# Inverse norms of the MLA latents: diagonal tiles made one or two products ahead of the matmuls that spread them

## The chip, the core and the metric

The kernel runs on one core of one Trainium2 chip. The metric is the device time of one launch in microseconds (us). The engines named here are PE (matrix multiply), DVE (vector), ACT (scalar), POOL (GpSimd) and SP, whose queue issues most of the DMAs. Each works through its own list of instructions in order and waits for the others by semaphores.

## The reference, cut to what matters

The program is one layer of a hybrid decoder over 1024 tokens of width 2048. An RMSNorm and one input projection feed three head groups: multi-head latent attention (MLA), native sparse attention (NSA) and cross-attention into 256 memory tokens. Their outputs go through SiLU gates, one output projection, the residual and a last RMSNorm.

What the change touches is a small piece of it. The projection yields two latents of 512 features per token, `c_q` and `c_kv`, and each is normalised before it is multiplied by its up-projection:

```python
def rmsnorm(x, g):
    xf = x.astype(jnp.float32)
    y = xf * lax.rsqrt(jnp.mean(xf * xf, axis=-1, keepdims=True) + EPS)
    return (y * g.astype(jnp.float32)).astype(x.dtype)

q = (rmsnorm(c_q, q_norm_g) @ w_uq).reshape(...)
kv = (rmsnorm(c_kv, kv_norm_g) @ w_ukv).reshape(...)
```

## The kernel before, in words

**The projection.** Activations lie transposed: 128 features on the partitions, 1024 tokens along the row. The projection is done in 20 units of two feature tiles each, twice (once for each half of the 2048 input rows, so 40 units `u`; the second half starts at `u0` = 20). A unit is a Strassen-like scheme of seven products `s` = 0..6. A product is 12 matmuls of 512 columns: four k-tiles, each three times, because every operand is split in a high and a low float32r part (`mm3`, L124 to L126). `wprep` makes the split weights of a product two products ahead in the units around the change: ACT writes the high part (L118), DVE the low one (L112), and POOL forms sums of weight blocks (L719 to L723). `evac` takes the product out of PSUM, by ACT (L756, L760) or DVE (L758 to L770). In the second half POOL then adds the first half's result by a DMA (`work<-part`).

**Work at the side.** Everything else is hung on the list of products with `at(u, s, ...)`: the functions given there are issued after product `s` of unit `u`. In this part the engines' lists keep the order in which the code issues instructions. Here that are a compression MLP for keys in 12 chunks (`kc_chunk`, matmuls into tile `J`, 66x384) and one for values in four (`vc_start`, `vc_prep`, `vc_chunk`, loads of `in_w1v`), and the norms of the latents.

**The norms.** `c_sum` adds up the squares of four feature tiles in `cacc[g]` (`g` = 0 for `c_q`, 1 for `c_kv`). `c_col` (`col_rsqrt`) lets PE sum them over the partitions by eight pairs of tiny matmuls with a matrix of ones (L202), and DVE and ACT turn the sums into 8 columns of inverse norms (L130 to L136): column `i` holds those of tokens 128i to 128i+127, one token on a partition. `c_spread` (`spread`) turns them back into a row that is the same on all partitions. For each column DVE multiplies the identity matrix by it, which gives a diagonal tile `dg` (L214), and PE multiplies ones by that tile (L215). A `dg` tile holds two diagonals, and there are two such tiles at a time. Four diagonals fill a PSUM tile `T` of 512 columns, ACT copies it (L216), and after both halves the row is stored (`rd[g]`), to be read again much later by `c_load`.

So `c_spread` of one latent is eight instructions on DVE and eight matmuls on PE in turn, all after one product: product 6 of unit `u0+4` for `c_q` and product 0 of unit `u0+7` for `c_kv`. The profile has two records for each of these matmuls. `spread` is used at two more places earlier in the program, for the input's and the memory's norms, which stay as they are.

Of the kernel before, what the change touches and what calls it, by code (L numbers as in the profile page):

```python
# [6 lines left out]
F32 = mybir.dt.float32  # L7
F32R = mybir.dt.float32r
AF = mybir.ActivationFunctionType
ALU = mybir.AluOpType  # L10
AX = mybir.AxisListType

P = 128
# [3 lines left out]
NQ = SEQ // P  # L17
# [35 lines left out]
def hybrid_block_kernel(ctx: ExitStack, tc, a, out):  # L53
    nc = tc.nc
    V, S, G, PE = nc.vector, nc.scalar, nc.gpsimd, nc.tensor

    cst = ctx.enter_context(tc.tile_pool(name="cst", bufs=1))
    sb = ctx.enter_context(tc.tile_pool(name="sb", bufs=1))
# [5 lines left out]
    def nm(s):  # L64
        uid[0] += 1
        return f"{s}_{uid[0]}"

    def big(dt=F32R):
        return sb.tile([P, 2048], dt, tag="big", bufs=16, name=nm("big"))
# [22 lines left out]
    def psT():  # L92
        return ps.tile([P, 512], F32, tag="T", bufs=2, name=nm("T"))
# [10 lines left out]
    def store(dst, src):  # L104
        nc.sync.dma_start(dst, src)
# [32 lines left out]
    def const(name, shape, dt=F32):  # L138
        t = cst.tile(shape, dt, tag=name, name=name)
        load(t, a[name])  # L140
        return t


    def dram(name, shape):
        return dr.tile(shape, F32, name=name)
# [5 lines left out]
    rd = [dram(f"r{j}", [P, SEQ]) for j in range(2)]  # L151
# [53 lines left out]
    def spread(dst, col, n, bank=None):  # L205

        for i0 in range(0, n, 4):
            t = (bank or psT)()
            m = min(4, n - i0)
            for j in range(i0, i0 + m, 2):  # L210
                dg = sb.tile([P, 256], F32, tag="og", bufs=2, name=nm("dg"))
                for i in (j, j + 1):
                    d = dg[:, (i - j) * P:(i - j) * P + P]
                    V.tensor_scalar(d, ident, col[:, i:i + 1], None, op0=ALU.mult)  # L214
                    PE.matmul(t[:, (i - i0) * P:(i - i0 + 1) * P], ones, d, start=True, stop=True)  # L215
            S.activation(dst[:, i0 * P:(i0 + m) * P], t[:, :m * P], AF.Copy)  # L216
# [114 lines left out]
    for c in range(8):  # L331
# [4 lines left out]
        for k in (2 * c, 2 * c + 1):  # L336
            g = ng[:, k:k + 1]
# [6 lines left out]
            else:  # L344
                xr = work()
                t = big()
                parts = [(t[:, :512], t[:, 1024:1536]), (t[:, 512:1024], t[:, 1536:])]
            if k == 0:
# [3 lines left out]
                ones = const("ones", [P, P])  # L352
                ident = const("ident", [P, P])
# [110 lines left out]
    def in_load(key):  # L464
        cmp_["in"] = slot(F32)[:, :1024]
        load(cmp_["in"], cmp_[key])
# [116 lines left out]
    cacc = {}  # L583
# [12 lines left out]
    ccol = {}  # L596

    def c_col(g):
        ccol[g] = small()
        col_rsqrt(ccol[g][:, :NQ], cacc[g], NQ, 512)  # L600

    def c_spread(g):
        spread(cacc[g], ccol[g], NQ)
        store(rd[g], cacc[g])

    def c_load(j):
        t = big(F32)
# [193 lines left out]
    def at(u, s, *fs):  # L801
        side.setdefault((u, s), []).extend(fs)
# [105 lines left out]
    for k in range(8):  # L908
        g = 28 + 13 * k
# [21 lines left out]
    u0 = NU  # L931
# [11 lines left out]
    for c in range(12):  # L943
# [7 lines left out]
        if c == 7:  # L951
            at(x // 7, x % 7, kc_rest)
    at(u0 + 4, 5, lambda: c_col(0))
    at(u0 + 4, 6, lambda: c_spread(0))
    at(u0 + 6, 4, w2_load)
    at(u0 + 6, 5, kc_mid)
    at(u0 + 6, 6, kc_mid2, lambda: in_load("vc"), lambda: c_col(1))
    at(u0 + 7, 0, lambda: c_spread(1))
    at(u0 + 7, 1, kc_end)
    at(u0 + 7, 0, lambda: vc_load(0))  # L960
    at(u0 + 7, 2, vc_start, lambda: vc_prep(0))
# [14 lines left out]
    for h in range(4):  # L976
        g = 64 + 18 * h
# [820 lines left out]
```

## Time and profile before

| | |
|---|---|
| median of 3 runs | 1905.29 us (1904.3 to 1909.41) |
| profiled execution, its own time | 1902.97 us |
| span of its trace, first to last instruction | 1901.2 us |
| PE busy | 1789.8 us, 94% of the span |
| DVE busy | 1319.8 us, 69% |
| ACT busy | 854.1 us, 45% |
| POOL busy | 320.3 us, 17% |
| mean clock granted to PE | 0.978 of full speed |

The trace is of one execution, and its own time is 2.3 us below the median of the runs. The share of busy time is an average over stages. PE counts as busy while a matmul is under way, whatever its clock. A granted clock of 1.00 is 2.4 GHz, and 0.50 is 1.2 GHz. In a row of the timeline the first two numbers are the start and the length in us. Matmuls overlap in the pipe, so that their pace is read from one start to the next, not from their length. What stands in brackets at a row's end is the time that the engine had idled before it and whose instruction ended that.

### The profile page before, as it was taken

The numbers are of one execution on the slowest core, as the hardware profiler recorded it, in microseconds if no ns is written. First come the engines' busy times: TensorE is split into PE (matmuls) and PEld (weight loads), VectorE is DVE, ScalarE is ACT, GpSimd is POOL, SyncE is SP. The second block draws the span as 40 slices with busy tenths as digits, with TensorE's granted clock in tenths as the row PEclk, the third lists the DMA queues.
The fourth block names the chain that finished last, engine by engine and source line by source line (L and its number), as shares of the span: only waits on it lengthen the run. The fifth ranks groups of instructions, "written<-read, shape, count | busy, mean of one in ns | idle before, by whom it ended". The sixth has DMA issues, their size and how long they took to land. (4 is left out here: it accounts for less than half of the span.)

```text
span 1901.2 us, 26461 instructions
## 1 busy us (share of the span) xinstructions
PE 1789.8 (94%) x9310; PEld 1525.8 (80%) x9310; DVE 1319.8 (69%) x2478; ACT 854.1 (45%) x1712; POOL 320.3 (17%) x433
## 2 busy tenths in 40 slices
PE   8899999999999889989897999999999999989996
PEld 7788878887777767778776898888999988877885
DVE  7976778877866545766664887868777783544777
ACT  8753222222434344534454666545455453222344
POOL 0002223223242213233231221200000000000020
PEclk9999999999999989999998999999999999999998
DMA  6564877786588558878988213442122144754564
GB/s 223 184 190 166 293 256 270 256 305 224 220 227 240 146 153 235 274 215 252 301 251 264 80 61 136 156 130 65 46 73 68 56 140 141 245 167 144 167 195 192
DMA packets 124930, 351.91 MB, mean 185 GB/s; under 512 B 15355, under 2 KB 39613, under 8 KB 121725
## 3 DMA queue, kind: packets, MB, share of 16 engines
q1 hardware_dynamic: 119037, 329.25, 51.4%
q0 software_dynamic: 5760, 20.97, 6.3%
q8 instruction: 73, 1.20, 0.3%
q14 instruction: 60, 0.49, 0.1%
HBM read 242.14 MB, written 108.02 MB: 184 GB/s over the span
## 5 line engine op out<-in xcount | busy, mean ns | idle before, releaser
L124 PE MATMUL S<-big,wh 128*128 128x512 f32 x1336 | 529.5, 396 | 23.1 <-DVE work L758 7.9
L125 PE MATMUL S<-big,wh 128*128 128x512 f32 x1336 | 526.6, 394 | 4.5 <-DVE big L112 4.5
L126 PE MATMUL S<-big,wh 128*128 128x512 f32 x1336 | 526.5, 394 | 1.4 <-DVE wh L112 1.2
L124 PEld LDWEIGHTS S<-big,wh 128*128 128x128 f32 x1336 | 254.7, 191 | 80.0 <-issue 12.1
L125 PEld LDWEIGHTS S<-big,wh 128*128 128x128 f32 x1336 | 254.8, 191 | 56.4 <-DVE big L112 6.0
L126 PEld LDWEIGHTS S<-big,wh 128*128 128x128 f32 x1336 | 253.9, 190 | 57.1 <-DVE wh L112 3.4
L112 DVE TENSOR_TENSOR wh<-wraw,wh 128x512 fp32r<-128x512 f32 (+2 forms) x226 | 201.2, 892 | 80.7 <-ACT wh L118 80.6
L118 ACT ACTIVATE wh<-wraw 128x512 fp32r<-128x512 f32 (+2 forms) x226 | 145.5, 659 | 92.7 <-PE S L126 44.8
L112 DVE TENSOR_TENSOR big<-wraw,big 128x1024 fp32r<-128x1024 f32 x56 | 73.9, 1320 | 104.6 <-ACT big L118 104.4
L719 POOL TENSOR_TENSOR wraw<-wraw 128x512 f32<-128x512 f32 x38 | 56.1, 1475 | 460.6 <-DMA wraw<-in_w_feat 415.8
L645 ACT ACTIVATE work<-S,st 128x512 f32<-128x512 f32 (+3 forms) x148 | 84.4, 572 | 86.4 <-DVE st L1096 35.2
L118 ACT ACTIVATE wh<-rs 128x512 fp32r<-128x512 f32 x80 | 50.2, 628 | 158.3 <-POOL rs L720 126.4
L112 DVE TENSOR_TENSOR wh<-rs,wh 128x512 fp32r<-128x512 f32 x80 | 62.7, 784 | 65.2 <-ACT wh L118 65.0
L118 ACT ACTIVATE big<-wraw 128x1024 fp32r<-128x1024 f32 x56 | 59.2, 1056 | 84.8 <-PE J L126 57.7
L124 PE MATMUL J<-big,wh 128*128 128x512 f32 x214 | 84.2, 393 | 0.7 <-ACT wh L118 0.7
L125 PE MATMUL J<-big,wh 128*128 128x512 f32 x214 | 84.1, 393 | 0.0
L126 PE MATMUL J<-big,wh 128*128 128x512 f32 x214 | 83.9, 392 | 0.0
L118 ACT ACTIVATE wh<-T 128x512 fp32r<-128x512 f32 (+2 forms) x112 | 53.0, 504 | 46.5 <-PE T L1161 29.5
L756 ACT ACTIVATE work<-S 128x512 f32<-128x512 f32 x40 | 23.8, 596 | 110.5 <-PE S L126 105.9
L112 DVE TENSOR_TENSOR wh<-T,wh 128x512 fp32r<-128x512 f32 (+2 forms) x112 | 61.5, 570 | 10.5 <-ACT wh L118 10.1
L1425 POOL MEMSET wh<- 128x128 f32 x64 | 13.8, 227 | 291.8 <-PE O L125 173.5
L1078 PE MATMUL S<-big,big 128*128 128x512 f32 (+2 forms) x144 | 52.9, 368 | 8.5 <-ACT wraw L645 8.5
(377 smaller groups left out, 4133.2 us busy)
## 6 DMA issues: line engine op xcount, KB each, us to landing
wraw<-in_w_feat SPq DMA_DIRECT2D x80, 512.0 KB, 5.3
part<-work SPq DMA_DIRECT2D x40, 512.0 KB, 3.9
work<-part POOLq DMA_DIRECT2D x40, 512.0 KB, 6.7
work<-og SPq DMA_DIRECT2D x72, 256.0 KB, 4.3
wh<-in_w_o SPq DMA_DIRECT2D x32, 512.0 KB, 7.2
t<-wh SPq DMA_DIRECT2D x32, 512.0 KB, 3.0
wraw<-t SPq DMA_DIRECT2D x32, 512.0 KB, 3.8
wraw<-in_w_o SPq DMA_DIRECT2D x24, 512.0 KB, 4.1
```

Of the source, the lines that this page charges most:

```text
L112: V.tensor_tensor(dst, src, f(hi), op=ALU.subtract)
L118: S.activation(hi, src, AF.Copy)
L124: PE.matmul(dst, sh, mh, start=start, stop=False, skip_group_check=shared)
L125: PE.matmul(dst, sh, ml, start=False, stop=False, skip_group_check=shared)
L126: PE.matmul(dst, sl, mh, start=False, stop=stop, skip_group_check=shared)
L645: S.activation(dst, src, AF.Exp, bias=m, scale=-1.0, accum_out=s)
L719: E.tensor_tensor(B12, B22, B12, op=ALU.subtract)
L756: S.activation(C21, B, AF.Copy)
L1078: PE.matmul(d, qm[0][:, c:c + P], km[0][:, k0:k0 + n], start=True, stop=False)
L1425: G.memset(f(t[:, o:o + P]), 0.0)
```

## The change

`c_spread` of the latents no longer calls `spread`. It is cut in two steps for each half of the row. `c_diag(g, half)` makes four diagonals in the two `dg` tiles. `c_spread(g, half)` multiplies ones by each `dg` tile as a whole (256 columns, one matmul in place of two of 128 columns) and copies the half row out. `c_spread(g, 0)` issues `c_diag(g, 1)` at its end, since the two `dg` tiles are free only then.

```diff
+    dgs = {}
+    def c_diag(g, half):
+        for j in (4 * half, 4 * half + 2):
+            dg = dgs[j] = sb.tile([P, 256], F32, tag="og", bufs=2, name=nm("dg"))
+            for i in (j, j + 1):
+                V.tensor_scalar(dg[:, (i - j) * P:(i - j) * P + P], ident, ccol[g][:, i:i + 1], None, op0=ALU.mult)
-    def c_spread(g):
-        spread(cacc[g], ccol[g], NQ)
-        store(rd[g], cacc[g])
+    def c_spread(g, half):
+        t = psT()
+        for j in (4 * half, 4 * half + 2):
+            PE.matmul(t[:, (j % 4) * P:(j % 4) * P + 256], ones, dgs.pop(j), start=True, stop=True)
+        S.activation(cacc[g][:, half * 512:half * 512 + 512], t, AF.Copy)
+        if half:
+            store(rd[g], cacc[g])
+        else:
+            c_diag(g, 1)
...
-    at(u0 + 4, 6, lambda: c_spread(0))
+    at(u0 + 4, 6, lambda: c_diag(0, 0))
+    at(u0 + 5, 0, lambda: c_spread(0, 0))
+    at(u0 + 5, 1, lambda: c_spread(0, 1))
...
-    at(u0 + 7, 0, lambda: c_spread(1))
+    at(u0 + 7, 0, lambda: c_diag(1, 0))
+    at(u0 + 7, 2, lambda: c_spread(1, 0))
+    at(u0 + 7, 4, lambda: c_spread(1, 1))
```

PE's list at the first place (`c_q`), before: the last matmuls of product 6 of unit `u0+4`, the spread (`T<-dg,ones`), and the first of the next product.

```order
L124 MATMUL S_5043<-big_4425,wh_5040 128x512
L125 MATMUL S_5043<-big_4426,wh_5040 128x512
L126 MATMUL S_5043<-big_4425,wh_5040 128x512
L215 MATMUL T_5133<-dg_5134,ones 128x128 x2
L215 MATMUL T_5133<-dg_5139,ones 128x128 x2
L215 MATMUL T_5145<-dg_5146,ones 128x128 x2
L215 MATMUL T_5145<-dg_5151,ones 128x128 x2
L124 MATMUL S_5163<-big_4216,wh_5065 128x512
```

The same place on PE after the change, from the end of the next product's chunk of the key MLP (`J`) on; between the two halves stand the 12 matmuls of product 1 of unit `u0+5`, of which the first and the last are shown.

```order
L126 MATMUL J_4788<-wh_5126,dl_4783 66x384
L613 MATMUL T_5169<-dg_5133,ones 128x256
L613 MATMUL T_5169<-dg_5136,ones 128x256
L124 MATMUL S_5184<-big_4257,wh_5109 128x512
...
L126 MATMUL S_5184<-big_4257,wh_5109 128x512
L613 MATMUL T_5202<-dg_5173,ones 128x256
L613 MATMUL T_5202<-dg_5176,ones 128x256
L124 MATMUL S_5144<-big_4302,wh_5139 128x512
```

The first half has moved behind one product and one chunk, the second behind one product more. DVE's list at that place, before: `wh<-big` is the low part of a chunk's weights, `wh<-wraw` that of a product's.

```order
L112 TENSOR_TENSOR wh_5127<-big_5037,wh_5126 128x768
L214 TENSOR_SCALAR dg_5134<-ident,st_5089 128x128 x2
L214 TENSOR_SCALAR dg_5139<-ident,st_5089 128x128 x2
L214 TENSOR_SCALAR dg_5146<-ident,st_5089 128x128 x2
L214 TENSOR_SCALAR dg_5151<-ident,st_5089 128x128 x2
L112 TENSOR_TENSOR wh_5158<-wraw_4942,wh_5158 128x512
```

And DVE's list at that place after the change.

```order
L112 TENSOR_TENSOR wh_5127<-big_5037,wh_5126 128x768
L608 TENSOR_SCALAR dg_5133<-ident,st_5089 128x128 x2
L608 TENSOR_SCALAR dg_5136<-ident,st_5089 128x128 x2
L112 TENSOR_TENSOR wh_5139<-wraw_4942,wh_5139 128x512
L608 TENSOR_SCALAR dg_5173<-ident,st_5089 128x128 x2
L608 TENSOR_SCALAR dg_5176<-ident,st_5089 128x128 x2
L112 TENSOR_TENSOR wh_5181<-wraw_5016,wh_5181 128x512
```

The first four diagonals stand where they stood, and one weight split has moved ahead of the other four. SP's list around the store of the second row (`r_134`), before: `wraw` are weight loads (`in_w_feat` for products, `in_w1v` for the value MLP), `rs<-km` and `rs<-vm` the memory keys and values, which reuse the buffer that this store reads.

```order
L102 DMA wh_5512<-vcraw 128x1024
L105 DMA r_134<-rs_5228 128x1024
L105 DMA kc<-wh_5597 128x256
L102 DMA rs_5879<-km 128x2x256
L102 DMA wraw_5644<-in_w_feat 128x1024
L102 DMA rs_5879<-vm 128x2x128 x2
L105 DMA qm_145<-big_5625 128x1024 x2
L102 DMA wraw_5671<-in_w1v 128x1024
L102 DMA wraw_5676<-in_w_feat 128x1024
L105 DMA qm_146<-big_5692 128x1024 x2
L102 DMA wraw_5750<-in_w1v 128x1024
```

SP's list at that place after the change.

```order
L102 DMA wh_5508<-vcraw 128x1024
L105 DMA kc<-wh_5574 128x256
L102 DMA wraw_5631<-in_w_feat 128x1024
L105 DMA qm_145<-big_5602 128x1024 x2
L102 DMA wraw_5658<-in_w1v 128x1024
L105 DMA qm_146<-big_5679 128x1024
L102 DMA wraw_5663<-in_w_feat 128x1024
L105 DMA r_134<-rs_5224 128x1024
L105 DMA qm_146<-big_5679 128x1024
L102 DMA rs_5871<-km 128x2x256
L102 DMA wraw_5742<-in_w1v 128x1024
L102 DMA rs_5871<-vm 128x2x128 x2
```

The store has moved behind four weight loads and two other stores, and the loads of the memory keys and values have moved with it; a load of the value MLP's weights now stands behind them.

## Rows read from the trace of the kernel before

**Rows 1.** The page: the span, and PE's busy time.
```profile
span 1901.2 us, 26461 instructions
PE 1789.8 (94%) x9310; PEld 1525.8 (80%) x9310; DVE 1319.8 (69%) x2478; ACT 854.1 (45%) x1712; POOL 320.3 (17%) x433
```
**Rows 2.** PE's waits, 600 to 720 us: total, times, longest in us.
```profile
PE T L215 <- DVE dg L214: 7.8, 3, 4.2
```
**Rows 3.** Timeline of PE at the first spread: start, length, engine, line, operation.
```profile
624.72 0.39 PE L125 MATMUL S<-big,wh 128*128 128x512 f32 x1
624.95 0.39 PE L126 MATMUL S<-big,wh 128*128 128x512 f32 x1
...
629.57 1.22 PE L215 MATMUL T<-dg,ones 128*128 128x128 f32 x4 [4.22 <-DVE dg L214]
...
630.97 2.93 PE L215 MATMUL T<-dg,ones 128*128 128x128 f32 x12 [0.18 <-DVE dg L214]
633.55 0.77 PE L124 MATMUL S<-big,wh 128*128 128x512 f32 x1
...
634.97 0.40 PE L124 MATMUL S<-big,wh 128*128 128x512 f32 x1
```
**Rows 4.** Busy time by stretch; after POOL's come granted clock, DMA share, GB/s.
```profile
629.50:635.00 5.50, 5.26 (x20) 4.67 (x21) 2.49 (x8) 1.67 (x3) 1.33 (x1) 0.50 0.65 98
635.00:640.00 5.00, 5.00 (x25) 4.05 (x24) 1.39 (x2) 2.42 (x5) 0.00 (x0) 1.00 0.53 210
...
690.60:696.60 6.00, 5.91 (x22) 5.45 (x23) 2.19 (x8) 1.71 (x3) 0.00 (x0) 0.51 0.19 63
```
**Rows 5.** Timeline of PE at the second spread.
```profile
686.95 0.39 PE L126 MATMUL S<-big,wh 128*128 128x512 f32 x1
690.69 3.76 PE L215 MATMUL T<-dg,ones 128*128 128x128 f32 x16 [3.35 <-DVE dg L214]
694.10 0.78 PE L124 MATMUL S<-big,wh 128*128 128x512 f32 x1
...
696.64 0.40 PE L124 MATMUL S<-big,wh 128*128 128x512 f32 x1
```
**Rows 6.** Timeline of PE at the input norms' spread: a half row, and what follows.
```profile
102.65 1.05 PE L215 MATMUL S<-dg,ones 128*128 128x128 f32 x8
103.46 0.36 PE L125 MATMUL O<-wh,wh 128*128 128x256 f32 x1
```
**Rows 7.** Timelines of DVE and POOL at the first spread.
```profile
627.73 1.78 DVE L214 TENSOR_SCALAR dg<-ident,st 128x128 f32<-128x128 f32 x1
...
629.43 1.48 DVE L214 TENSOR_SCALAR dg<-ident,st 128x128 f32<-128x128 f32 x2
...
630.84 0.27 DVE L214 TENSOR_SCALAR dg<-ident,st 128x128 f32<-128x128 f32 x1
...
627.85 1.57 POOL L722 TENSOR_TENSOR wraw<-wraw,rs 128x512 f32<-128x512 f32 x1
629.50 1.33 POOL L723 TENSOR_TENSOR rs<-wraw,rs 128x512 f32<-128x512 f32 x1
```
**Rows 8.** Timelines of ACT and PE before the first chunk of the value MLP.
```profile
702.43 0.60 ACT L760 ACTIVATE work<-S 128x512 f32<-128x512 f32 x1 [2.20 <-PE S L126]
...
706.99 0.33 PE L124 MATMUL J<-wh,dh 128*66 128x256 f32 x1 [1.88 <-ACT wh L118]
709.10 0.34 PE L125 MATMUL J<-wh,dh 128*66 128x256 f32 x1 [1.77 <-DVE wh L112]
```
**Rows 9.** SP's waits 660 to 702, r store's landing, SP's and ACT's timelines.
```profile
SPq L105 <- ACT rs L216: 16.8, 1, 16.8
...
DMA to landing us min/median/max: 2.6/2.6/2.6
...
719.52 10.58 SPq L102 DMA_DIRECT2D wraw<-in_w1v  x2
...
726.58 1.58 ACT L118 ACTIVATE wh<-wraw 128x1024 fp32r<-128x1024 f32 x2 [0.93 <-DMA wraw<-in_w1v]
```

## The prediction, as put on record before the changed kernel ran

> **What bounds the kernel now.** I read the page's busy times first, then PE's waits around the code that changes, then the timelines at both places, and the granted clock there. PE is busy for 94% of the span [rows 1], so what counts is where PE stands still or runs slowly. Between 600 and 720 us, which hold both spreads, its largest wait by far is that of the spreading matmuls for DVE's diagonals, 7.8 us in three pieces [rows 2].
>
> At the first place PE's last product matmul starts at 624.95. PE then idles 4.22 us, because DVE's first diagonal comes only at 629.5, and waits another 0.18 us within the spread [rows 3]. The idling has a second price. From 629.5 to 635 the granted clock is 0.50 (1.2 GHz), and it is 1.00 (2.4 GHz) from 635 on [rows 4]. The next product starts at 633.55, and three of its matmuls pass before the full pace is back at 634.97 [rows 3]. The second place is the same with 3.35 us of waiting [rows 5] and a clock of 0.51 [rows 4]; six product matmuls pass from 694.10 until the full pace is back at 696.64 [rows 5].
>
> **What each place costs beyond its work.** A product matmul takes 0.23 us at full clock (624.72 to 624.95 [rows 3]). The input norms are spread elsewhere at full clock without a wait: four diagonals, eight records, take 0.81 us (102.65 to 103.46 [rows 6]), so eight take 1.62.
> - First place: 624.95 to 634.97 is 10.02 us. It holds four product matmuls (0.92) and the spread (1.62), which is 2.54. Lost: 7.48 us.
> - Second place: 686.95 to 696.64 is 9.69 us. It holds seven product matmuls (1.61) and the spread (1.62), which is 3.23. Lost: 6.46 us.
>
> Together 13.9 us are lost, the most that there is to get back directly.
>
> **The change, part by part.** *Diagonals made ahead, first place.* DVE's list is unchanged up to the fourth diagonal, so the first four come when they came: the first ends at 629.51, the second one 0.27 us after its start at 629.43, so at 629.70, the third at 629.43 + 1.48 = 630.91 and the fourth at 631.11 [rows 7]. The first took 1.78 us, the second and third together 1.48, the fourth 0.27, and both long ones ended within 0.1 us of a POOL instruction (627.85 + 1.57 = 629.42, and 629.50 + 1.33 = 630.83). POOL's list doesn't change either, and what it waits for comes as before, so I expect the same collision. What changes is what PE does meanwhile: product 0 of unit u0+5 (12 x 0.23 = 2.76) and a chunk of the key MLP (6 matmuls of 384 columns, by the width 0.17 each, 1.04; its weights are split just ahead of the diagonals). From 624.95 + 0.23 = 625.18 that carries PE to 628.98. It waits 0.7 us for the first tile, does half of the first half row (0.41), and waits until 631.11, another 1.0. So about 1.7 us of the 7.48 remain, in two short pieces, and 5.8 are gained. The bounds are nothing left (7.5 gained), if DVE and POOL don't meet, and the old clock loss on top of 1.7, which I take up as a rival.
>
> The Trainium skill, SBUF — State Buffer, section "Who interferes with whom", bears on this: a tensor_scalar on DVE can take the port pair that DVE shares with GpSimd, and the one that comes second is blocked for the other's whole instruction. By it the diagonals stay late however early PE's list wants them, as long as POOL's two sums run there, and 5.8 stands; by accident alone it would be 7.5. The two long diagonals, ending with POOL's sums, agree with the rule.
>
> *Wider matmuls.* No row shows a plain float32 matmul of 256 columns. Its cost for a half row is bounded below by two one-pass matmuls of half the 512-column price, 2 x 0.12 = 0.23 us (first row pair of [rows 3]), and above by the 0.81 us of the four narrow ones [rows 6]. I take 0.81, the row for the same values in the same type. The lower end would give back 4 x 0.58 = 2.3 us more. The Trainium skill, FP8 and Floating Point Precision, section "TensorE Precision Notes", says that true FP32 takes four passes; an estimate by that page is that 256 columns cost four times the one-pass price whatever the cut, and the sum stays.
>
> *The second four diagonals.* They wait for PE to have read the first two tiles, and behind them on DVE stand a weight split and the evacuation of the product before. At the first place PE is through with the first half at about 631.5. DVE arrives there after the one split that now stands ahead (0.7 us from 631.1), so it hardly waits, and the four diagonals (some 0.2 us apart) are done long before PE's next product ends at 634.3. At the second place they fall behind 2 products of slack. Cost: nothing; the cover is PE's product between the halves, 2.76 us, against about 1 us of diagonals.
>
> *Second place.* The first half now comes behind products 1 and 2 of unit u0+7. The first diagonal let PE go at 690.69 [rows 5], and three more at 0.3 each are there by 691.6; two products alone carry PE from 687.18 to 692.7, and the end of the key MLP comes on top: no wait is left, and all 6.46 us go. Next late is the first chunk of the value MLP. PE idles there 1.88 + 1.77 us, and this wait runs from the evacuation of product 2 (702.43) over a chain on ACT and DVE to 709.10 [rows 8]. The first half row (0.81 us) now lies inside that wait, and its copy lengthens ACT's chain by about 0.5 (0.60 long, as L760, and slightly overlapped). That is 0.3 us gained, 6.8 at this place. The wait's own clock loss stays as it is.
>
> *Store and loads on SP.* SP stood 16.8 us on the store of the second row, with a chain of other transfers behind it, and PE paid nothing for that. The store now stands behind them and is ready some 1.5 us after PE's second half; it landed in 2.6 us [rows 9]. The load of the memory keys must wait for that landing, and behind it is a load of the value MLP's weights that has no slack: it was issued at 719.52, and ACT idled 0.93 us for it until 726.58 [rows 9]. Store and landing fit before the moment when that load's buffer is free, so the order costs no wait by my reckoning; the two loads of memory tokens now run beside it. Bounds: 0, and 2.6 if the landing is waited for in full. I take 0.5, near the lower row.
>
> **Sum.** 5.8 + 6.8 - 0.5 = 12.1 us off. All later transfers and splits hang on PE's own progress (buffers freed, products evacuated), so I expect the lead to be kept. Against the profiled execution's 1902.97 that gives 1890.9. It lies 2.3 us below the median of the runs, so the median goes from 1905.29 to **1893.2**.
>
> **Rivals.**
> - *The clock stays low at the first place.* Two waits of 0.7 and 1.0 us with 0.41 us of work between might let the clock fall, as 4.22 us did. For it: the fall follows a wait at both places. Against: the wait is shorter and broken. The price is half of the 5.5 us at clock 0.50, 2.7 us: 9.4 off, **1895.9**.
> - *The lead is taken back in the value MLP.* If the DMAs for its chunks, and not PE's progress, set when they run, the second place's gain turns into longer waits for them. For it: ACT already idled for in_w1v [rows 9]. Against: each of these loads waits for a buffer that PE's progress frees. Only the first place is left, 5.8 off less what the second adds: **1899.5**.
> - *SP's list stalls the weights, and it gets slower.* The store waits for ACT's copy of the second half, and a value-MLP load, then product weights, stand behind it. If that store holds the list as long as it did before, 16.8 us [rows 9], these weights come as late, and PE with them: 16.8 - 12.1 = 4.7 us slower, **1910**. From a hold of 12.1 us on it decides. Against: the copy now follows PE's second half at once.
>
> **Chances.** Forecast 0.68, clock 0.14, value MLP 0.13, SP 0.05. About 0.3% (5.7 us) is what a measurement of this kernel can tell from no change, so the border is at 1899.6. The forecast, the clock case and half of the value-MLP case lie below it: faster 0.88. The other half and a mild SP case are within 0.3%: 0.08. Slower: 0.04. The range: the most that can come back is 13.9 + 0.3, which is 1891, and the lowest run lay 1 us under the median: 1890. Upward it reaches the value-MLP case, 1900.
>
> **What would show it.** Right: no wait of PE for dg at the second place, two waits of about 1 us at the first, a clock of 1.00 from 625 to 640 and in the spreads; product 2 of unit u0+5 starting about 5.8 us earlier, and the first chunk of the value MLP about 12.6 earlier (from 709.10). Wrong: a clock of 0.5 at the first place; DVE idle ahead of the second diagonals with PE waiting for a weight split behind them; PE's waits in the value MLP longer by microseconds; or a lead at 710 that is gone by 960.

## The result and the profile after

The changed kernel took 1894.14 us (median of 8 runs, the lowest 1891.17) against 1904.8 us before (median of 8 runs beside it, the lowest 1901.68); the ratio is 0.9939 with a 95% interval of 0.9924 to 0.9955. By the ratio that is 11.6 us faster; 12.1 were forecast. One of the eight runs, at a granted clock of 0.84, took 1998.84 us and is not in the ratio. The page of the profile after has these rows for [rows 1].

```profile
span 1891.1 us, 26430 instructions
PE 1786.8 (94%) x9294; PEld 1523.0 (81%) x9294; DVE 1317.0 (70%) x2478; ACT 854.9 (45%) x1712; POOL 323.8 (17%) x433
```

PE's busy time fell by only 3.0 us of the span's 10.1: most of what went was standing still. PE's waits between 600 and 720 us (total, times, longest) show where, beside [rows 2].

```profile
PE J L125 <- DVE wh L112: 6.0, 6, 1.8
PE J L124 <- ACT wh L118: 1.5, 1, 1.5
PE T L613 <- DVE dg L608: 1.4, 2, 0.7
```

The waits for diagonals are 1.4 us instead of 7.8, both at the first place. The timeline of PE there answers to [rows 3].

```profile
629.62 0.33 PE L126 MATMUL J<-wh,dl 128*66 128x384 f32 x1
630.65 0.70 PE L613 MATMUL T<-dg,ones 128*128 128x256 f32 x2 [0.70 <-DVE dg L608]
632.05 0.70 PE L613 MATMUL T<-dg,ones 128*128 128x256 f32 x2 [0.70 <-DVE dg L608]
632.40 0.58 PE L124 MATMUL S<-big,wh 128*128 128x512 f32 x1
...
635.11 0.39 PE L126 MATMUL S<-big,wh 128*128 128x512 f32 x1
635.34 1.02 PE L613 MATMUL T<-dg,ones 128*128 128x256 f32 x4
```

The key MLP's chunk ends first; the first tile of two diagonals is waited for, then the second; after one product the other half row runs without a wait. The busy times by stretch (after POOL's come the granted clock, the DMA share and GB/s) answer to [rows 4].

```profile
625.00:629.50 4.50, 4.50 (x23) 3.62 (x22) 3.83 (x5) 2.44 (x4) 2.21 (x3) 1.00 0.51 104
629.50:634.00 4.50, 3.10 (x14) 2.02 (x13) 3.95 (x10) 1.26 (x4) 2.14 (x2) 1.00 1.01 220
634.00:640.00 6.00, 6.00 (x29) 4.90 (x28) 2.88 (x4) 2.36 (x4) 0.00 (x0) 1.00 0.59 209
688.00:694.00 6.00, 5.70 (x26) 4.37 (x24) 3.10 (x9) 3.89 (x5) 0.00 (x0) 1.00 0.61 215
694.00:697.00 3.00, 0.33 (x1) 0.13 (x1) 2.93 (x3) 3.00 (x6) 0.00 (x0) 0.88 0.36 143
697.00:705.00 8.00, 7.74 (x28) 6.69 (x29) 2.79 (x6) 0.09 (x1) 0.00 (x0) 0.62 0.62 197
```

The clock stays at 1.00 (2.4 GHz) through the first place and the first half of the second, where it was 0.50 and 0.51 (1.2 GHz). From 694 to 697, where PE waits for the value MLP's first chunk, it is 0.88, and behind these waits 0.62. The timeline of PE at the second place answers to [rows 5, 8].

```profile
689.91 1.02 PE L613 MATMUL T<-dg,ones 128*128 128x256 f32 x4
690.58 0.58 PE L124 MATMUL S<-big,wh 128*128 128x512 f32 x1
...
695.16 0.33 PE L124 MATMUL J<-wh,dh 128*66 128x256 f32 x1 [1.46 <-ACT wh L118]
697.26 0.48 PE L125 MATMUL J<-wh,dh 128*66 128x256 f32 x1 [1.77 <-DVE wh L112]
```

The half row takes no wait. The chunk behind it waits 1.46 and 1.77 us (1.88 and 1.77 before). The timelines of DVE and then POOL answer to [rows 7].

```profile
628.61 3.39 DVE L608 TENSOR_SCALAR dg<-ident,st 128x128 f32<-128x128 f32 x4
```

```profile
628.73 1.58 POOL L736 TENSOR_TENSOR wraw<-wraw,rs 128x512 f32<-128x512 f32 x1
630.39 1.33 POOL L737 TENSOR_TENSOR rs<-wraw,rs 128x512 f32<-128x512 f32 x1
```

The four diagonals still take 3.39 us beside the same two sums. SP's wait for the row's store (685 to 715 us), SP's timeline behind the second place and ACT's wait for the weights (700 to 745 us) answer to [rows 9].

```profile
SPq L105 <- ACT rs L614: 6.3, 1, 6.3
```

```profile
705.71 0.32 SPq L105 DMA_DIRECT2D r<-rs  x1
...
708.41 0.59 SPq L102 DMA_DIRECT2D rs<-km  x1
709.70 0.34 SPq L102 DMA_DIRECT2D wraw<-in_w1v  x1
```

```profile
ACT wh L118 <- DMA wraw<-in_w1v: 1.3, 1, 1.3
```

The row's store held SP for 6.3 us instead of 16.8. It now goes out behind three of the four stores of memory queries and behind three weight loads (the section on the change says four); the load of the keys follows 2.7 us after it, and the weights for the value MLP next. ACT waits 1.3 us for them (0.93 before).

To see where the time came off, I match PE's matmuls of two kernels one by one; the *lead* is a matmul's start in before less its start in the other kernel. Each row is one profiled execution; the columns are the matmul's start in before. Only differences within a row count: the lead at 623 lies ahead of every edit and is scatter. The profiled executions of e8 (1898.67 us) and e12 (1893.03) were the slowest of their six.

| kernel | 623 | 642 | 660 | 679 | 716 | 737 | 748 | 1000 | 1890 |
|---|---|---|---|---|---|---|---|---|---|
| after | -0.87 | 4.62 | 4.15 | 4.19 | 9.84 | 9.78 | 7.16 | 11.50 | 10.32 |
| after again (e15) | 2.69 | 8.17 | 7.72 | 7.75 | 13.04 | 13.02 | 10.81 | 15.15 | 12.45 |
| e1 | -1.72 | 3.74 | 3.30 | 3.34 | 4.74 | 4.70 | 2.12 | 2.41 | 3.16 |
| e2 | 0.17 | 0.64 | 0.64 | 0.66 | 5.99 | 5.98 | 3.63 | 4.77 | 4.65 |
| e3 | 0.21 | 0.37 | 0.39 | 0.39 | 0.81 | 0.82 | 0.68 | 0.98 | 0.81 |
| e4 | -3.39 | 2.25 | 1.78 | 1.80 | 8.74 | 8.54 | 6.77 | 7.58 | 7.39 |
| e5 | 0.02 | 1.66 | 1.67 | 1.70 | 4.13 | 4.12 | 4.18 | 6.90 | 5.06 |
| e6 | -3.43 | 3.96 | 0.44 | 0.46 | 6.03 | 6.03 | 5.95 | 7.47 | 6.46 |
| e7 | -1.12 | 6.30 | 3.36 | 3.39 | 8.41 | 8.40 | 6.39 | 9.33 | 9.43 |
| e8 | -2.48 | 3.01 | 2.54 | 2.55 | 12.77 | 11.39 | 7.68 | 7.03 | 4.31 |
| e10 | -0.23 | 7.16 | 7.13 | 7.14 | 15.48 | 15.46 | 13.26 | 17.63 | 17.67 |
| e12 | 1.12 | 8.51 | 8.50 | 8.52 | 18.74 | 17.40 | 18.58 | 12.82 | 9.93 |
| e14 | 3.82 | 10.17 | 10.15 | 10.15 | 20.89 | 19.29 | 20.91 | 15.55 | 13.42 |

After gains 5.49 at the first place (623 to 642), gives 0.47 back at the key MLP's next chunk (by 660), gains 5.65 at the second (679 to 716), gives 2.62 back at the value MLP's last chunk (737 to 748) and gains 3.16 over all the rest: 11.2 in all. These 3.16 have come by 830 us: two waits of PE for the memory attention's weights, 0.89 and 0.53 us in before, are gone (1.17 and 0.74 gained), a wait for a product's evacuation is 0.68 longer, and two more waits of the memory attention take 2.92 us instead of 4.85 (1.94 gained).

### The profile page after: what moved, and what is told of

Its sections match the earlier page's. It is cut to its first block, busy times and chain, and to the rows that moved or that the text cites. A ratio compares the mean times of both kernels' runs of the same rounds, so it can differ in the third digit from the quotient of the medians.

```text
span 1891.1 us, 26430 instructions
## 1 busy us (share of the span) xinstructions
PE 1786.8 (94%) x9294; PEld 1523.0 (81%) x9294; DVE 1317.0 (70%) x2478; ACT 854.9 (45%) x1712; POOL 323.8 (17%) x433
```

## Experiments

Ratios are to the kernel before, run on the same chip: 1904.76 us (26 runs) for e1 to e4, 1905.14 (12) for e5 to e8, 1904.43 (11) for e10 to e15.

**e1: the first place alone.** From the changed kernel, with c_kv spread as before:

```diff
-    at(u0 + 7, 0, lambda: c_diag(1, 0))
+    at(u0 + 7, 0, lambda: c_spread_old(1))
-    at(u0 + 7, 2, lambda: c_spread(1, 0))
-    at(u0 + 7, 4, lambda: c_spread(1, 1))
```

> The change at the first place (c_q) alone; the second latent is spread as before. Theory (the time comes from PE's waits for the diagonals and the clock they cost, place by place): 5.5 us off, about 1899.3, with two waits of PE for dg of about 0.7 us and a clock of 1.00 there. Rival (the gain comes from fewer and wider matmuls, wherever they stand): half of the whole gain too, so the time alone does not tell the two apart, but the third kernel does. Rival (the value MLP takes a lead back): the whole 5.5 us are still there at the end, since this lead arises before that MLP, or they shrink by up to 2 us between 700 and 750 us.

1901.24 us, ratio 0.9976 (0.9962 to 0.9991). The first place gains 5.46 as in the whole change, 0.44 goes at the same key chunk, and 2.58 at the value MLP's last chunk although nothing near it was moved.

**e2: the second place alone.** The same for c_q:

```diff
-    at(u0 + 4, 6, lambda: c_diag(0, 0))
+    at(u0 + 4, 6, lambda: c_spread_old(0))
-    at(u0 + 5, 0, lambda: c_spread(0, 0))
-    at(u0 + 5, 1, lambda: c_spread(0, 1))
```

> The change at the second place (c_kv) alone. Theory: 5.6 to 6.8 us off, about 1898.5; no wait of PE for the diagonals there; the first chunk of the value MLP still waits for ACT and DVE and runs at a lower clock. Rival (wide matmuls): the same time. Rival (SP's new order holds loads back): less than 4 us off, with longer waits of PE in the value MLP than in the kernel before.

1899.61 us, ratio 0.9964 (0.995 to 0.9977); 5.33 gained at the second place. The ratios of e1 and e2 multiply to 0.9940, the whole change's 0.9939: the places add.

**e3: wide matmuls, nothing moved.**

```diff
-    at(u0 + 5, 0, lambda: c_spread(0, 0))
-    at(u0 + 5, 1, lambda: c_spread(0, 1))
+    at(u0 + 4, 6, lambda: c_spread(0, 0))
+    at(u0 + 4, 6, lambda: c_spread(0, 1))
```

and likewise both halves of c_kv at (u0 + 7, 0).

> The wide matmuls alone: one 256-column matmul per diagonal tile, but all diagonals and matmuls of a latent in one go after the same product as before. Theory: no gain; PE's first wait grows by the second diagonal of a tile (0.2 to 0.3 us), the same waits of 4.2 and 3.4 us and the clock of 0.50 stay; within 1.5 us of the kernel before. Rival (wide matmuls are the gain): 6 us off or more.

1906.09 us, ratio 1.0003 (0.9989 to 1.0017). PE's waits (600 to 720 us):

```profile
PE T L613 <- DVE dg L608: 7.0, 4, 4.5
```

The width alone leaves the waits and the time as they were.

**e4: moved, but narrow matmuls.**

```diff
-            PE.matmul(t[...:... + 256], ones, dgs.pop(j), ...)
+            dg = dgs.pop(j)
+            for n in (0, P):
+                PE.matmul(t[...:... + P], ones, dg[:, n:n + P], ...)
```

> The changed kernel with the old narrow matmuls: everything is moved as in the change, but each diagonal tile is multiplied in two matmuls of 128 columns. Theory: as the changed kernel within 0.5 us in its trace (11 us off by its ratio), since four narrow matmuls at full clock cost 0.81 us and two wide ones 0.86. Rival (wide matmuls): 5 us less gain.

1897.25 us, ratio 0.9955 (0.9939 to 0.9971). The places gain 5.64 and 6.94, no less than with wide ones. By the traces the move is the effect; e3's interval leaves the width at most 2.1 us.

**e5: the waits of before, filled.** The old order, with matmuls that nobody reads in PE's two idle stretches (more work, for the clock alone):

```diff
+        t = psT()
+        for n in range((20, 16)[g]):
+            PE.matmul(t, XH[0][:, :P], XH[0][:, 512:1024], start=True, stop=True)
         spread(cacc[g], ccol[g], NQ)
```

> The kernel before, with PE's two waits filled: 20 (first place) and 16 (second) extra matmuls of 512 columns, whose result nobody reads, stand between the last product matmul and the spread. They take 0.23 us each, 4.5 and 3.6 us, about as long as the waits. Theory (the wait costs twice, as a wait and as a low clock after it): the clock stays 1.00 through both spreads, so 2.2 us at the first place and 2.8 at the second come back while the waits themselves stay, together 4.5 to 5 us off, about 1900. Rival (the low clock comes from the spreading matmuls themselves, not from the wait ahead of them): the clock is still 0.50 in the spreads, and the time is that of the kernel before within 1 us, or slower.

1899.61 us, ratio 0.997 (0.9959 to 0.9981). Busy times by stretch, the clock third from the end:

```profile
625.00:629.50 4.50, 4.50 (x22) 3.67 (x20) 3.86 (x5) 1.35 (x2) 2.20 (x2) 1.00 0.62 159
629.50:635.00 5.50, 4.87 (x29) 3.99 (x28) 3.19 (x9) 1.71 (x3) 1.33 (x1) 1.00 0.71 153
...
689.00:694.00 5.00, 5.00 (x32) 4.34 (x30) 2.12 (x8) 1.71 (x3) 0.00 (x0) 1.00 0.31 114
```

With PE kept busy the clock stays at 1.00 where before had 0.50 and 0.51, and 1.64 and 2.43 us come off at the two places: the low clock came from the wait, and it was three tenths of the 13.9 us that the places lost.

**e6: c_q's diagonals at once behind their column.**

```diff
-    at(u0 + 4, 5, lambda: c_col(0))
-    at(u0 + 4, 6, lambda: c_diag(0, 0))
+    at(u0 + 4, 5, lambda: c_col(0), lambda: c_diag(0, 0))
```

> The changed kernel with the first four diagonals of c_q issued one product earlier, straight after the inverse norms, where POOL is idle. Theory (the 1.4 us that PE still waits at the first place come from two of POOL's sums that run beside DVE's diagonals): the four diagonals take 0.28 us each, both waits are gone, and the trace gains 1.4 us at the first place over the changed kernel, before losses elsewhere; by time 11 to 13.5 us off the kernel before. Rival (DVE's own order makes the diagonals late): the waits stay, same time as the changed kernel.

1893.94 us, ratio 0.994 (0.9926 to 0.9953): no better than after. The two waits are gone and the first place gains 7.39 instead of 5.49, but 3.52 are given back by 660. ACT's timeline and then SP's show how:

```profile
642.25 1.06 ACT L590 ACTIVATE rs<-work 128x1024 f32<-128x1024 f32 x1 [1.82 <-DMA r<-rs]
```

```profile
630.68 7.40 SPq L105 DMA_DIRECT2D c<-work  x2
638.17 0.38 SPq L105 DMA_DIRECT2D r<-rs  x1
```

The first square of c_kv goes to a buffer of the tag rs, which the store of c_q's row still reads; that store stands on SP behind one of c that is held 7.40 us. ACT waits, the split for the key chunk behind it is late, PE waits 0.76 + 1.47 us there, and the clock falls to 0.62 (648 to 652 us). After has the same wait with 0.32 us, and PE waits 0.97 us for that chunk's weights (0.55 before); there it cost the 0.47.

**e7: the diagonals on ACT.**

```diff
-                V.tensor_scalar(dg[...], ident, ccol[g][:, i:i + 1], None, op0=ALU.mult)
+                S.activation(dg[...], ident, AF.Copy, scale=ccol[g][:, i:i + 1])
```

> The changed kernel with the diagonals made by ACT (a copy of the identity with the column as scale) in place of DVE, at the same places of the list. Theory (DVE and POOL get in each other's way, ACT and POOL do not): the diagonals take about 0.25 to 0.35 us each although POOL's two sums run at the same time; PE's two waits of 0.7 us at the first place go; 11 to 13.5 us off the kernel before. Rival (the diagonals are slow because of their own operands): long ones remain, and PE still waits 1.4 us.

1891.72 us, ratio 0.9927 (0.9914 to 0.994). The tile's rows (duration in ns: least, median, most), then the timelines of ACT, POOL and DVE:

```profile
L608 ACT ACTIVATE dg<-ident,st x16: 384/392/402, 627.4 to 693.7; 128x128 f32<-128x128 f32 x16
```

```profile
627.39 1.27 ACT L608 ACTIVATE dg<-ident,st 128x128 f32<-128x128 f32 x4
...
631.60 1.27 ACT L608 ACTIVATE dg<-ident,st 128x128 f32<-128x128 f32 x4
```

```profile
628.98 1.58 POOL L736 TENSOR_TENSOR wraw<-wraw,rs 128x512 f32<-128x512 f32 x1
630.64 1.63 POOL L737 TENSOR_TENSOR rs<-wraw,rs 128x512 f32<-128x512 f32 x1
```

```profile
629.21 1.91 DVE L112 TENSOR_TENSOR wh<-wraw,wh 128x512 fp32r<-128x512 f32 x1 [0.27 <-ACT wh L118]
```

All sixteen last the same; on DVE the longest took 1.80 us and the median 0.28. The first four run ahead of POOL's sums (by 1.59 us; DVE started 0.12 us ahead in after), so PE's two waits go because ACT comes to the diagonals sooner. That ACT is not held up beside a sum is shown by the second four alone, three of which run beside POOL's second sum. DVE now has a weight split there, which takes 1.91 us instead of 0.69; PE shows no wait for it. The first place gains 7.42, as in e6, and 2.94 go at the same key chunk, where ACT waits 2.87 us for the store of c_q's row.

**e8: the value MLP's first chunk one product later.**

```diff
-    at(u0 + 7, 4, lambda: c_spread(1, 1))
+    at(u0 + 7, 3, lambda: c_spread(1, 1))
-    at(u0 + 7, 3, lambda: vc_chunk(0), lambda: vc_load(1))
+    at(u0 + 7, 3, lambda: vc_load(1))
+    at(u0 + 7, 4, lambda: vc_chunk(0))
```

> The changed kernel with the first chunk of the value MLP one product later and the second half row of c_kv one product earlier. Theory (what is late next is that chunk: PE idles 1.46 + 1.77 us for it and then runs 3 us at half clock): the product that now stands ahead of it covers 2.7 of the 3.2 us, the clock stays at 1.00, and 4 to 5 us more come off: 15 us off the kernel before, about 1890. Rival (the chain on ACT and DVE moves along with the chunk, or SP's loads take it back in the later chunks): the lead after this chunk is gone by 750 us, same time as the changed kernel.

1892.46 us, ratio 0.9931 (0.9913 to 0.995). The chunk's wait goes, the clock is 1.00 from 690 to 712 us, and the second place gains 10.2. By 748 us 5.1 are given back: the MLP's last chunk waits 1.64 + 1.12 us, and the clock is 0.50 from 732 to 736. The 1890 expected were not reached: of the 4.5 us that this trace is ahead of after's at 716 us, 2.1 are left at 748, much as the rival has it.

**e10: e6, and the row in a tile of its own.**

```diff
-        S.activation(cacc[g][:, half * 512:half * 512 + 512], t, AF.Copy)
+        if half == 0:
+            crow[g] = slot(F32)[:, :1024]
+        S.activation(crow[g][:, half * 512:half * 512 + 512], t, AF.Copy)
-            store(rd[g], cacc[g])
+            store(rd[g], crow[g])
```

> As e6 (diagonals of c_q at once behind their column), and the spread row of each latent goes to a tile of its own, so that the sums of c_kv need not wait until the store of c_q's row has read the old one. Theory (what e6 gave back at the key MLP came through that buffer): the ACT wait of 1.8 us before c_kv's first square is gone, the key MLP's chunk behind it no longer waits 0.76 + 1.47 us, the clock there stays 1.00, and the lead at 660 us is about 3.5 us above e6's (some 4.0 instead of 0.44); the end 2 to 3.5 us earlier, about 1891. Rival (the chunk waits for its own weights whatever the squares do): the wait before the square goes, the chunk's waits stay, the time is e6's 1894.

1884.66 us, ratio 0.9902 (0.9882 to 0.9922), the fastest of all. The same square, in ACT's timeline:

```profile
637.12 1.05 ACT L590 ACTIVATE rs<-work 128x1024 f32<-128x1024 f32 x1
```

It waits for nothing, the key chunk waits 0.53 us, and of the 7.39 gained only 0.03 go by 660. So e6's give-back came through that buffer. Against e15 the means of six runs each differ by 7.0 us (95% interval 3 to 11). Of these the trace shows 2.3 at the first place and key chunk; 3 more are the second place (8.34 against 5.29), where the clock fell neither ahead of the spread nor behind the chunk this time; that this comes from the edit is not shown.

**e12: e10, and two value chunks later.** As e8, and besides

```diff
-    at(u0 + 8, 5, lambda: vc_chunk(3))
-    at(u0 + 8, 6, vc_mid)
-    at(u0 + 9, 0, vc_mid2)
+    at(u0 + 8, 6, lambda: vc_chunk(3))
+    at(u0 + 9, 0, vc_mid, vc_mid2)
```

> As e10, with the value MLP's chunk 0 one product later as in e8 and its chunk 3 one product later too. Theory (at both chunks TensorE only waits for weights that are not split yet): chunk 0 runs without a wait and the clock stays 1.00 to 712 us (5 us more at the second place, as in e8), chunk 3 waits under 0.5 us instead of 1.6 + 1.1 and the clock stays 1.00 there, so that what e8 gave back by 748 us (5 us) is kept: about 1887. Rival (the lead is given back wherever the list of loads on SP is late, because a transfer sets the pace there and not the order of the products): the lead falls by as much behind 720 us at another wait, time 1892 as e8.

1887.67 us, ratio 0.9912 (0.989 to 0.9935). Both chunks wait under 0.8 us, and of the lead of 18.74 at 716 us 18.58 stand at 748. Then PE's and ACT's timelines:

```profile
733.44 0.66 PE L513 MATMUL O<-cin,big 66*128 66x64 f32 x4 [3.43 <-ACT big L566]
```

```profile
731.51 1.13 ACT L118 ACTIVATE wh<-wraw 128x512 fp32r<-128x512 f32 x2
732.55 0.58 ACT L772 ACTIVATE work<-S 128x512 f32<-128x512 f32 x1
733.02 0.36 ACT L566 ACTIVATE big<-J 66x256 f32<-66x256 f32 x1
```

My edit put the copy of the MLP's result and the matmul that reads it in one place; the copy stands behind splits on ACT, PE waits 3.43 us, and the lead is 13.3 at 760. The edit repeats the mistake that the change mends. Another 3.7 us go between 1000 and 1030 us, where PE waits 2.56, 0.60 and 2.47 us for three loads; before waits there only for the last, 2.18 us. The unaltered change loses 2.55 in the same stretch in e15 (1.84, 0.36 and 1.52 us for the same loads) and 0.09 in its first profile, so this need not come from the edit. A version with the two apart was not run.

**e14: e12 with the diagonals on ACT** (e7's edit).

> As e12, with all 16 diagonals on ACT instead of DVE. Theory (a diagonal on DVE is late only where POOL's sums run beside it): 16 diagonals of 0.39 us on ACT, no long ones; since e10's order already hides the long ones behind a product, the gain over e12 is small, 0 to 1 us: about 1886.5. Rival (ACT is the engine that feeds the weights of both MLPs, so 6 us more on it delay them): chunk waits grow by 0.5 to 1 us each at the two or three chunks near by, and the time is 1 to 3 us above e12.

1890.51 us, ratio 0.9936 (0.9914 to 0.9959). The same 3.4 us wait; the two places gain 6.35 and 10.7 (e12: 7.39 and 10.2). The intervals of e12 and e14 overlap, so which engine is better here is not settled; ACT brings nothing that shows.

**e15: the change once more.**

> The change itself once more, unaltered, on the same chip as the three kernels beside it, so that they can be set against it there. All theories: a ratio to the kernel before of 0.994, within 0.9925 to 0.9955; two waits of 0.7 us for diagonals, 1.5 and 1.8 us before chunk 0 and 1.7 and 1.1 us before chunk 3 of the value MLP. If those waits differ by over 0.5 us in this second profile, differences of that size between the other kernels prove nothing.

1891.92 us, ratio 0.9938 (0.9917 to 0.9959); the six named waits agree with the first profile but for the last chunk's first, 1.45 against 1.70. The clock does not agree. Busy times of the 8 us behind the second wait of the value MLP's first chunk, of e10, e15 and after:

```profile
694.30:702.30 8.00, 7.99 (x41) 6.87 (x42) 4.36 (x7) 2.40 (x4) 0.00 (x0) 1.00 0.79 269
```

```profile
695.40:703.40 8.00, 8.00 (x35) 7.04 (x36) 3.89 (x6) 1.51 (x3) 0.00 (x0) 0.81 0.62 202
```

```profile
697.30:705.30 8.00, 8.00 (x29) 6.91 (x30) 2.79 (x5) 0.22 (x1) 0.00 (x0) 0.64 0.62 197
```

Three executions with the same waits there, 1.46 and 1.77 or 1.78 us: the clock behind them is 1.00 in e10, 0.81 in e15 and 0.64 in after.

## Why the prediction was right, step by step

- **First place, 5.8 forecast, 5.49 measured** (5.46 in e1, 5.48 in e15). The two remaining waits were put at 0.7 and 1.0 and are 0.70 each. They cost 1.9 us and not 1.4: from the key chunk's last matmul to the next product are 2.78 us in after (629.62 to 632.40), and 0.85 in e7 (629.87 to 630.72), which has no wait there. The mechanism behind them holds: the diagonals are long only on DVE beside POOL's sums. The upper bound given for DVE and POOL not meeting, 7.5, is what e6 and e7 reach, with 7.39 and 7.42. The Trainium skill, SBUF — State Buffer, section "Who interferes with whom", says that DVE's instruction and GpSimd's exclude each other at the shared port pair. The traces agree: 1.80 us beside POOL's sum, 0.28 us without, and 0.39 us on ACT beside one of the sums. The first long diagonal starts 0.12 us ahead of POOL's sum in both kernels, so the traces don't show which of the two comes first.
- **Clock at the first place.** The rival (two short waits bring the clock down) is wrong: 1.00 throughout. The price of the old fall was real: e5 got 1.64 us back there without moving anything.
- **Wide matmuls.** 0.81 us were taken for a half row; its records run from 689.91 to the next product at 690.58, and 0.88 us, a little over the upper bound of 0.81, is what the lead falls by where a half row was moved in. The lower bound of 0.23 is excluded, and e3 and e4 show that the width is worth nothing that can be measured.
- **Second four diagonals.** No wait, as forecast.
- **Second place, 6.8 forecast, 5.65 measured.** The wait for diagonals is gone and the value chunk's shorter by 0.4 (0.3 forecast). The mis-sized term is "the wait's own clock loss stays as it is": in that chunk and behind it the lead falls by another 0.78 + 0.32 us, because the clock stayed low for longer than before. It is not a fixed loss: over six executions with the new second place and the same two waits (after, e2, e4, e6, e10, e15), the place gains between 5.3 (e15) and 8.3 us (e10). One part is the clock ahead of the spread: with the half rows still to come, the lead has grown by 8.13 us at 700 in after, e4, e6, e7, e10 and e14, and by 6.5 in e2, e8, e12 and e15, where the clock fell shortly before the spread. So e15's 5.29 and after's 5.65 are different sums that come out alike by chance.
- **Key chunk, not foreseen.** 0.47 us went through the store of c_q's row, its buffer and ACT. I had counted what the store delays on SP at the second place, and not who reuses the buffer that it reads at the first.
- **SP and the weights, 0.5 forecast.** The wait for the weights grew by 0.3 us, near the forecast, and the store held SP for 6.3 us; the larger loss is at the value MLP's last chunk, 1.05 us of waiting more and a clock of 0.73 and 0.85 behind it where before had 1.00: 2.6 us. ACT stood 6.6 us there for a buffer that a store of memory queries reads (5.5 before). These are the rows of SP and ACT, before and then after:

```profile
731.54 1.58 SPq L105 DMA_DIRECT2D qm<-big  x2
738.10 1.06 ACT L120 ACTIVATE big<-work 128x1024 fp32r<-128x1024 f32 x1 [5.55 <-DMA qm<-big]
```

```profile
721.72 1.59 SPq L105 DMA_DIRECT2D qm<-big  x2
729.36 1.06 ACT L120 ACTIVATE big<-work 128x1024 fp32r<-128x1024 f32 x1 [6.63 <-DMA qm<-big]
```

  From the store's issue to ACT's restart are 6.56 us before and 7.64 after. The loss goes with this time: the time is 6.5 to 6.7 us in before, e3, e5 and e6, and these three lose at most 0.14; it is 6.9 to 7.6 us in after, e1, e2, e4, e7, e10 and e15, which lose 1.8 to 2.6, the clock's fall included. e1 has SP's old order, so the moved row store is not the cause; why the transfer takes longer stays open. The rival by which the value MLP takes back the second place named the DMAs for its chunks; what came is this store, 2.6 us of 5.65, and without the second place too (e1).
- **SP's list makes it slower.** Wrong: the store held SP for 6.3 us, under the 12.1 from which it decides; it goes out at 705.71 and the keys' load 2.7 us later.
- **The rest.** "The lead is kept" holds on the whole: 7.16 at 748, 10.32 at the end. The 3.16 us between were not forecast and vary between two profiles of the same kernel (1.64 in e15). They lie at PE's waits for the memory attention, and why these shrank is not explained; they happen to make up for the last chunk.

So the total is right by its two large terms, and in part by luck: smaller errors of both signs (-0.3 at the first place, -0.5 at the key chunk, -1.1 at the second place, -2.6 at the last chunk, where 0.5 was allowed for SP, and +3.2 behind it) nearly cancel. The 13.9 us called the most to get back were no ceiling: e10's trace gains 17.9, of them 8.34 at the second place, since the clock loss behind the value chunk went as well.

## What to carry to other kernels

Where TensorE waits for tiles that another engine makes from a result just computed, order the making one piece of work ahead of the use: what is won is the wait and the clock that it costs. Then look at who reuses the buffer that the moved step fills or stores from: making the diagonals earlier still gave 3.5 us back through such a buffer, and a tile of its own for the row kept them. And never put a producer and its reader back to back on the in-order lists while fixing another place, as e12 did.

## What the runs showed of the hardware

- A 128x128 tensor_scalar of 0.28 us on DVE took 1.80 us beside a 1.58 us sum on POOL and 1.28 us beside one of 1.33 us; a 128x512 weight split of 0.69 us took 1.91 beside them (e7). On ACT the same tile took 0.39 us beside a sum of 1.63 us (three tiles in e7).
- Behind equal waits of TensorE, 1.5 and 1.8 us with one matmul between, the granted clock over 8 us was 1.00, 0.81 or 0.64 in three executions. Behind two waits of 0.70 it stayed at 1.00, and behind one of 4.22 it was 0.50. So a microsecond of clock loss after a wait of a few is not a constant to build a sum on.
- In e15 the clock was also 0.74 and 0.83 from 676 to 684 us, behind the latent's column sums (sixteen matmuls of two columns, 1.95 us); in after it is 1.00 from 676 to 692. It cost 1.65 us of lead there.
